# One lo in four of the first mixer's early weight chunks moved from VectorE to GpSimd

## The chip, the cores and the metric

The kernel runs on one core of one Trainium2 chip. The metric is the device time of one execution in microseconds (us); the time before is the median of three runs. The profile is one further execution, with its own time.

## What is computed

A trunk of two layers over 256 positions of width 2048, batch 1, all in float32. Layer 0 mixes tokens with gated DeltaNet heads and band attention behind one combined input projection; layer 1 with a Mamba-2 SSD. Each layer ends in a squared-ReLU MLP, and all norms are modulated by vectors made from `c`.

```python
def reference(x, c, mod_w, mod_b, norm_mix_w, norm_mlp_w, mlp_w1, mlp_w2, ab_w_in, ...):
    c_act = jax.nn.silu(c)
    for layer in range(DEPTH):
        mod = jnp.einsum('bd,de->be', c_act, mod_w[layer]) + mod_b[layer]
        sh1, sc1, g1, sh2, sc2, g2 = [m[:, None, :] for m in jnp.split(mod, 6, axis=-1)]
        h = rms_norm(x, norm_mix_w[layer]) * (1.0 + sc1) + sh1
        ...
        x = x + g1 * mix
        h = rms_norm(x, norm_mlp_w[layer]) * (1.0 + sc2) + sh2
        x = x + g2 * sq_relu_mlp(h, mlp_w1[layer], mlp_w2[layer])
    return x

def gdn_attn_mixer(h, w_in, ...):
    proj = jnp.einsum('btd,de->bte', h, w_in)
    gq, gk, gv, gz, gb, ga, aq, ak, av = split_sizes(proj, AB_SPLITS)
    ...
```

The change lies in the product `proj` of layer 0.

## The kernel before

Every weight comes in chunks of 128x2048 float32 (1 MB) into one of four buffers `raw`. A product at nearly full float32 precision is made of three matmuls of the fast type fp32r: each operand is split into hi (the value rounded to fp32r) and lo (the value minus hi), and hi by hi, hi by lo and lo by hi are summed. `split` (line 317) makes the two: hi (`wh`) is a cast on ScalarE (line 318), lo (`wl`) a subtraction of two SBUF tensors (line 319). `loader` (line 467) issues a chunk's DMA on the SP queue (line 477) and splits its two halves, `hf` 0 and 1, of 128x1024 each. A buffer `raw` is free again when lo of both halves is done. The halves' tiles `wh` and `wl` have four buffers each.

`b_item` (line 496) and `a_item` (line 522) are one chunk's work: load and split at once, its matmuls (line 309) one item later, first those of half 0, then those of half 1. In `b_item` the weights are the stationary operand, in `a_item` the activations `u`.

The first mixer's input projection begins at line 1422. The width of 2048 is taken in four quarters `kg`, and in each of the first three the loop at line 1484 runs over eight chunks, n = 0 to 7 (`kinds`, line 1422: six `b_item`, then two `a_item`). The partial results of n = 0 and 1 stay in PSUM over all quarters; those of n = 2 to 7 are copied out by ScalarE in kg 0 (line 1439) and in kg 1 and 2 added to what is there by VectorE (line 1441, one operand in PSUM). Quarter 3 follows in another order from line 1497, with the rest of the mixer around it.

Between the chunks the modulation of layer 0 is computed: `mod_job` (line 419) loads eight chunks `mraw` per quarter into the same four buffers, through the same SP queue (line 430), and VectorE multiplies each by `crow` and sums (line 433). At the end of a quarter `norm_unit` (line 737) makes the next quarter's activations from them: VectorE (line 750), ScalarE (line 752), VectorE (line 753). In quarter 2 ScalarE makes an undivided copy as well (line 755).

Each engine runs its instructions in the order that the program's scheduler has laid down; it goes by the order of the source and by priorities (`mod_job` lowers that of its product). GpSimd makes masks at the start and clears small tiles later.

Of the kernel before, what the change touches and what calls it, by code (L numbers as in the profile page):

```python
# [10 lines left out]
F32 = mybir.dt.float32  # L11
# [3 lines left out]
ALU = mybir.AluOpType  # L15
# [97 lines left out]
class Trunk:  # L113
# [200 lines left out]
    def tr(self, o, a, k=P):  # L314
        self.nc.tensor.transpose(o, a, self.ident[:k, :k])  # L315

    def split(self, src, hi, lo, pin=False):
        a = self.nc.scalar.copy(hi, src)  # L318
        b = self.nc.vector.tensor_tensor(lo, src, hi.bitcast(F32), op=ALU.subtract)  # L319
        if pin:  # L320
            self.tc.keep_in_program_order(a)
            self.tc.keep_in_program_order(b)
# [141 lines left out]
                return  # L464


    def loader(self, src, whole=False):

        nc = self.nc
        if self.ahead:  # L470
            res, self.ahead = self.ahead[1], None
            return (lambda: None), res
        res = []

        def load():
            raw = self.raw_p.tile([P, 2048], F32, tag="raw", name=self.nm("raw"))
            nc.sync.dma_start(raw, src)
            for hf in range(2):
                r = raw[:, 1024 * hf : 1024 * hf + 1024]
                if whole:  # L480
                    res.append((r, None))
                    continue
                wh = self.w_p.tile([P, 1024], F32R, tag="wh", name=self.nm("wh"))
                wl = self.w_p.tile([P, 1024], F32R, tag="wl", name=self.nm("wl"))
                self.split(r, wh, wl, self.pin > 0)
                res.append((wh, wl))
            self.pin -= 1

        return load, res
# [3 lines left out]

        return [[w and w.rearrange("p (k c) -> p k c", c=width) for w in half] for half in ws]

    def b_item(self, ps, src, act, first, last, after=None, whole=False):

        load, ws = self.loader(src, whole)

        def run():  # L500
            o_, (u, x) = ps(), act()
            for hf, (wh, wl) in enumerate(self.tiles(ws, 512)):
                for ct in range(4):
                    o = o_[ct // 2][:, ct % 2, :]
                    cs = slice(ct * P, ct * P + P)
                    for k in range(2):
                        ka = hf * 2 + k
                        st = first and ka == 0 and ct % 2 == 0
                        sp = last and ka == 3 and ct % 2 == 1
                        if whole:  # L510
                            self.mmx(o, wh[:, k, cs], x[hf][:, k], st, sp)
                            continue
                        self.mmx(o, wh[:, k, cs], u[hf][:, k, 0], st, False)
                        self.mmx(o, wh[:, k, cs], u[hf][:, k, 1], False, False)
                        self.mmx(o, wl[:, k, cs], u[hf][:, k, 0], False, sp)
                    if ct % 2:
                        yield

        self.emit(Item(load, run, after, self.still > 0))
        self.still -= 1  # L520

    def a_item(self, ps, src, act, first, last, after=None, whole=False):

        load, ws = self.loader(src, whole)
        flip = self.flip and not whole

        def run():
            o_, (u, x) = ps(), act()
            for hf, (wh, wl) in enumerate(self.tiles(ws, 512)):
                if flip:  # L530
                    for k in range(2):
                        ka = hf * 2 + k
                        st, sp = first and ka == 0, last and ka == 3
                        T = [slice(t * P, t * P + P) for t in range(2)]
                        for n in range(3):
                            for t in range(2):
                                self.mmx(o_[t], u[hf][:, k, n // 2, T[t]], (wh, wl, wh)[n][:, k], st and n == 0, sp and n == 2)
                        yield
                    continue
                for n in range(4):  # L540
                    k, t = (n % 2, n // 2) if last and hf else (n // 2, n % 2)
                    ka = hf * 2 + k
                    ts = slice(t * P, t * P + P)
                    st = first and ka == 0
                    sp = last and ka == 3
                    o = o_[t]
                    if whole:
                        self.mmx(o, x[hf][:, k, ts], wh[:, k], st, sp)
                    else:
                        self.mmx(o, u[hf][:, k, 0, ts], wh[:, k], st, False)  # L550
                        self.mmx(o, u[hf][:, k, 0, ts], wl[:, k], False, False)
                        self.mmx(o, u[hf][:, k, 1, ts], wh[:, k], False, sp)
                    if n % 2:
                        yield

        self.emit(Item(load, run, after, self.still > 0))
        self.still -= 1
# [828 lines left out]
    def run(self):  # L1386
# [14 lines left out]
        first = self.mod_job(0, (0, 1), range(0, 4), 2)  # L1401
        for n, _ in enumerate(first):
            if n == 5:
                r = self.norm_r()
# [11 lines left out]
        w = i["w_ab"]  # L1416
# [10 lines left out]
        def unit_now(kg):  # L1427
            if len(acts) <= kg:
                self.flush()
            return acts[kg]  # L1430

        def partial(n, ps):
            first = parts[n] is None
            if first:
                parts[n] = self.unit(shape=[P, 2, 512])
            for b in range(2):
                o = ps[b].rearrange("p f t -> p (f t)") if len(ps[b].shape) == 3 else ps[b]
                if first:
                    nc.scalar.copy(parts[n][:, b], o)
                else:  # L1440
                    nc.vector.tensor_tensor(parts[n][:, b], o, parts[n][:, b], op=ALU.add)  # L1441
                if b == 0:
                    yield

        def last(n, ps):
            c0, kind = kinds[n]
            part = parts[n]
            if kind:
                return self.att_qk(ps, self.knw if c0 == AK else self.qnw, part)
            return self.conv(ps, {GK: 8, GQ: 0, GV: 16}[c0 // 2 * 2] + 4 * (c0 % 2), self.gconv, None,  # L1450
                             None if part is None else part.rearrange("p a (f t) -> p (a f) t", f=2))

        def partial_item(kg, n, then=None):
            c0, kind = kinds[n]
            ps = held[n] if n < 2 else []

            def psum():
                if not ps and n < 2:
                    ps.extend([self.pm([P, 2, SEQ]), self.pm([P, 2, SEQ])])
                if not ps:  # L1460
                    self.room()
                    ps.extend(self.pg(kind > 0))
                return ps

            def after():
                if kg < 3:
                    if n >= 2:
                        self.evac(partial(n, ps))
                else:
                    tasks[n].task = self.evac(last(n, ps))  # L1470
                if then:
                    then()

            (self.a_item if kind else self.b_item)(psum, w[kg, c0], lambda: unit_now(kg), n >= 2 or kg == 0, n >= 2 or kg == 3, after, kg == 3 and n > 2)

        for kg in range(3):
            self.modgen = self.mod_job(0, (0, 1), range(4 * kg + 4, 4 * kg + 8), 2)
            self.rate = 0.5

            def then(kg=kg):  # L1480
                self.pump(100)
                self.q(self.norm_unit(self.R, kg + 1, mix0, acts, kg == 2))

            for n in range(8):
                partial_item(kg, n, then if n == 6 else None)
# [9 lines left out]
        self.prep = [Flag(), Flag()]  # L1495
        gdn = []
        partial_item(3, 0)
        partial_item(3, 1)
        self.a_block(w, AV, get, lambda ps: put("v0", self.att_v(ps)))
        partial_item(3, 2)  # L1500
# [39 lines left out]
        w = i["w_ssd"]  # L1540
# [116 lines left out]
```

## Time and profile before

| | us |
|---|---|
| three runs, median | 2752.32 |
| their lowest and highest | 2750.8, 2754.2 |
| the profiled execution | 2751.96 |
| its span in the profile | 2750.2 |
| TensorE, matmuls busy | 2678.6 (97%) |
| VectorE busy | 2154.5 (78%) |
| ScalarE busy | 1323.7 (48%) |
| GpSimd busy | 24.6 (1%) |

Busy times are shares of the span of one execution; they run beside each other. Two instructions of one engine can overlap at their edges, so a pair is shorter than twice one. PE is TensorE, PEld its weight loads, DVE VectorE, ACT ScalarE, POOL GpSimd, SPq the queue of SyncE, which issues loads. An entry in brackets, or behind the bar, is time in which the engine stood idle ahead of the instruction, and what released it. L319 is line 319.

### The profile page before, as it was taken

The numbers are of one execution on the slowest core, as the hardware profiler recorded it, in microseconds if no ns is written. First come the engines' busy times: TensorE is split into PE (matmuls) and PEld (weight loads), VectorE is DVE, ScalarE is ACT, GpSimd is POOL, SyncE is SP. The second block draws the span as 40 slices with busy tenths as digits, with TensorE's granted clock in tenths as the row PEclk, the third lists the DMA queues.
The fourth block names the chain that finished last, engine by engine and source line by source line (L and its number), as shares of the span: only waits on it lengthen the run. The fifth ranks groups of instructions, "written<-read, shape, count | busy, mean of one in ns | idle before, by whom it ended". The sixth has DMA issues, their size and how long they took to land.

```text
span 2750.2 us, 39612 instructions
## 1 busy us (share of the span) xinstructions
PE 2678.6 (97%) x15610; PEld 2341.0 (85%) x15610; DVE 2154.5 (78%) x3211; ACT 1323.7 (48%) x1841; POOL 24.6 (1%) x98
## 2 busy tenths in 40 slices
PE   5999999999999999999999999999999999999999
PEld 5887989878888888888788888888878888888888
DVE  7998998988888888777889876898777755555555
ACT  3444454445355354454555544555445354354452
POOL 1000000000000000000000000000000000000000
PEclk9999999999999999999999999999999999999999
DMA  9986487869888888887456565656557755555554
GB/s 345 351 322 238 158 317 274 310 235 348 307 323 303 318 301 306 303 305 273 179 197 206 210 214 199 235 193 219 196 186 287 275 192 191 184 185 192 190 188 134
DMA packets 99306, 680.06 MB, mean 247 GB/s; under 512 B 11056, under 2 KB 12336, under 8 KB 18224
## 3 DMA queue, kind: packets, MB, share of 16 engines
q1 hardware_dynamic: 94224, 669.07, 67.3%
q10 hardware_dynamic: 4896, 8.46, 1.0%
q8 instruction: 123, 2.02, 0.3%
q14 instruction: 63, 0.52, 0.1%
HBM read 675.33 MB, written 2.16 MB: 246 GB/s over the span
## 4 chain that ended last, share of the span: by engine, by line
PE 91%; DVE 6%; ACT 1%; issue 1%; DMA 1%; ACTq 0%; SPq 0%; DVEq 0%
PE pw L309 71%; PE pg L309 13%; PE pm L312 4%; PE pm L309 3%; DVE mraw L433 2%; DVE wl L319 1%; PE pm L315 1%; DVE hf L750 1%; DVE u L753 0%; DVE u L1441 0%; DVE x L791 0%; ACT pm L904 0%; ACT wh L318 0%; DMA x<-in_x_dram 0%; DMA sd_rowd<-sd_rows 0%
## 5 line engine op out<-in xcount | busy, mean ns | idle before, releaser
L309 PE MATMUL pw<-u,wh 128*128 128x512 f32 x5632 | 1746.1, 397 | 9.2 <-DVE u L753 5.5
L318 ACT CAST wh<-raw 128x1024 fp32r<-128x1024 f32 x870 | 910.7, 1053 | 1097.7 <-PE pw L309 818.1
L319 DVE TENSOR_TENSOR wl<-raw,wh 128x1024 fp32r<-128x1024 f32 x870 | 1054.6, 1222 | 410.8 <-ACT wh L318 361.7
L309 PE MATMUL pw<-u,wl 128*128 128x256 f32 x5632 | 1185.4, 281 | 1.3 <-DVE wl L319 1.3
L309 PEld LDWEIGHTS pw<-u,wh 128*128 128x128 f32 x5632 | 990.4, 189 | 170.0 <-issue 10.6
L309 PEld LDWEIGHTS pw<-u,wl 128*128 128x128 f32 x5632 | 966.9, 190 | 93.9 <-DVE wl L319 2.6
L433 DVE SCALAR_TENSOR_TENSOR mraw<-mraw,crow 128x2048 f32<-128x2048 f32 x192 | 438.9, 2287 | 33.3 <-DMA mraw<-in_mod_dram 33.1
L309 PE MATMUL pg<-wh,u 128*128 128x512 f32 x864 | 269.7, 396 | 0.0
L791 DVE SCALAR_TENSOR_TENSOR x<-pw,mod,x 128x256 f32<-128x256 f32 x352 | 161.5, 480 | 70.1 <-PE pw L309 67.3
L309 PEld LDWEIGHTS pg<-wh,u 128*128 128x128 f32 x864 | 161.3, 188 | 31.9 <-issue 0.5
L309 PE MATMUL pg<-wl,u 128*128 128x512 f32 x432 | 159.9, 394 | 0.7 <-DVE wl L319 0.5
L309 PE MATMUL pg<-u,wh 128*128 128x256 f32 x672 | 124.6, 285 | 0.0
L309 PEld LDWEIGHTS pg<-u,wh 128*128 128x128 f32 x672 | 105.7, 192 | 0.3
L309 PEld LDWEIGHTS pg<-wl,u 128*128 128x128 f32 x432 | 81.2, 188 | 17.6 <-DVE wl L319 1.8
L309 PE MATMUL pg<-u,wl 128*128 128x256 f32 x336 | 95.2, 283 | 0.0
L309 PE MATMUL pm<-u,wh 128*128 128x256 f32 x256 | 47.7, 290 | 19.2 <-ACT wh L318 19.2
L309 PEld LDWEIGHTS pg<-u,wl 128*128 128x128 f32 x336 | 64.4, 192 | 0.1
L846 DVE SCALAR_TENSOR_TENSOR u<-pad,cst,u 128x256 f32<-128x256 f32 x144 | 61.3, 481 | 1.9 <-ACT u L840 1.8
L319 DVE TENSOR_TENSOR u<-rl,u 128x512 fp32r<-128x512 f32 x64 | 44.2, 690 | 21.6 <-ACT u L318 21.6
L309 PEld LDWEIGHTS pm<-u,wh 128*128 128x128 f32 x256 | 41.0, 198 | 20.2 <-ACT wh L318 20.0
L752 ACT ACTIVATE u<-hf,mod 128x256 fp32r<-128x256 f32 x64 | 29.8, 505 | 56.2 <-DVE hf L750 56.2
L1355 ACT COPY rs<-pw 128x512 f32<-128x512 f32 x64 | 37.3, 583 | 31.8 <-PE pw L309 31.8
(279 smaller groups left out, 1508.6 us busy)
## 6 DMA issues: line engine op xcount, KB each, us to landing
raw<-in_w_dram SPq DMA_DIRECT2D x256, 1024.0 KB, 5.0
mraw<-in_mod_dram SPq DMA_DIRECT2D x192, 1024.0 KB, 5.5
raw<-in_w_ab_dram SPq DMA_DIRECT2D x56, 1024.0 KB, 5.8
raw<-in_w_ssd_dram SPq DMA_DIRECT2D x48, 1024.0 KB, 4.9
raw<-in_w_sz_dram SPq DMA_DIRECT2D x32, 1024.0 KB, 4.9
raw<-in_wo_ssd_dram SPq DMA_DIRECT2D x32, 1024.0 KB, 4.8
raw<-in_wo_ab_dram SPq DMA_DIRECT2D x16, 1024.0 KB, 5.6
sE<-sd_rowd ACTq DMA_DIRECT2D x32, 256.0 KB, 5.0
```

What stands on the lines that cost most here:

```text
L309: self.nc.tensor.matmul(o, a, b, start=start, stop=stop, skip_group_check=True)
L312: self.nc.tensor.matmul(o, lhsT, rhs, start=True, stop=True, skip_group_check=True)
L315: self.nc.tensor.transpose(o, a, self.ident[:k, :k])
L318: a = self.nc.scalar.copy(hi, src)
L319: b = self.nc.vector.tensor_tensor(lo, src, hi.bitcast(F32), op=ALU.subtract)
L433: x = nc.vector.scalar_tensor_tensor(raw, raw, 1.0, self.crow, op0=ALU.mult, op1=ALU.mult, accum_out=t[:, f : f + 1])
L750: nc.vector.scalar_tensor_tensor(h[:, f], self.x[cb][:, ff], scale[:, col], r, op0=ALU.mult, op1=ALU.mult)
L752: nc.scalar.activation(hi, h[:, f], AF.Identity, bias=shift[:, col])
L791: nc.vector.scalar_tensor_tensor(x[:, 2 * b + f], ps[:, f, n], g[:, 2 * cb + f : 2 * cb + f + 1], x[:, 2 * b + f], op0=ALU.mult, op1=ALU.add)
L846: nc.vector.scalar_tensor_tensor(h, pad[:, f, 1 + q : 257 + q], w[:, q, j : j + 1], h, op0=ALU.mult, op1=ALU.add)
L1355: nc.scalar.copy(lo, ps[:, :, 1])
```

## The change

In the quarters kg 0 to 2, for odd n, the subtraction that makes lo of the second half (hf 1) is issued on GpSimd and no longer on VectorE: four chunks in each quarter, twelve instructions in all. What is computed stays the same.

```diff
-    def split(self, src, hi, lo, pin=False):
+    def split(self, src, hi, lo, pin=False, pool=False):
         a = self.nc.scalar.copy(hi, src)
-        b = self.nc.vector.tensor_tensor(lo, src, hi.bitcast(F32), op=ALU.subtract)
+        b = (self.nc.gpsimd if pool else self.nc.vector).tensor_tensor(lo, src, hi.bitcast(F32), op=ALU.subtract)
...
-    def loader(self, src, whole=False):
+    def loader(self, src, whole=False, pool=False):
...
-                self.split(r, wh, wl, self.pin > 0)
+                self.split(r, wh, wl, self.pin > 0, pool and hf == 1)
...
-    def b_item(self, ps, src, act, first, last, after=None, whole=False):
-
-        load, ws = self.loader(src, whole)
+    def b_item(self, ps, src, act, first, last, after=None, whole=False, pool=False):
+
+        load, ws = self.loader(src, whole, pool)
...
-            (self.a_item if kind else self.b_item)(psum, w[kg, c0], lambda: unit_now(kg), n >= 2 or kg == 0, n >= 2 or kg == 3, after, kg == 3 and n > 2)
+            (self.a_item if kind else self.b_item)(psum, w[kg, c0], lambda: unit_now(kg), n >= 2 or kg == 0, n >= 2 or kg == 3, after, kg == 3 and n > 2, kg < 3 and n % 2 == 1)
```

`a_item` takes and passes `pool` as `b_item` does.

## Rows read from the trace of the kernel before

**Rows 1.** The page: engine totals, and the chain that ended last by engine.
```profile
PE 2678.6 (97%) x15610; PEld 2341.0 (85%) x15610; DVE 2154.5 (78%) x3211; ACT 1323.7 (48%) x1841; POOL 24.6 (1%) x98
...
PE 91%; DVE 6%; ACT 1%; issue 1%; DMA 1%; ACTq 0%; SPq 0%; DVEq 0%
```

**Rows 2.** Windows kg 0, 1, 2: length, engines' busy us (instructions), TensorE clock, DMA share, GB/s.
```profile
40.10:87.90 47.80, 47.68 (x336) 45.32 (x336) 39.73 (x46) 21.48 (x31) 0.00 (x0) 1.00 0.93 349
89.70:137.00 47.30, 46.16 (x336) 43.58 (x337) 45.51 (x54) 19.22 (x23) 0.00 (x0) 1.00 0.92 349
137.00:185.10 48.10, 46.44 (x338) 43.64 (x337) 47.46 (x60) 18.68 (x22) 0.00 (x0) 1.00 0.93 350
```

**Rows 3.** The chain in order of time, end of kg 2: start, us, what.
```profile
180.86 1.20 DVE u L1441 x2
...
186.76 11.29 PE pm L309 x92
```

**Rows 4.** VectorE's groups, 89.7 to 185.1 us: count, busy, mean ns, idle before.
```profile
L319 DVE TENSOR_TENSOR wl<-raw,wh 128x1024 fp32r<-128x1024 f32 x32 | 37.7, 1221 | 1.0 <-ACT wh L318 0.6 <-issue 0.3
L433 DVE SCALAR_TENSOR_TENSOR mraw<-mraw,crow 128x2048 f32<-128x2048 f32 x16 | 36.6, 2285 | 0.4 <-DMA mraw<-in_mod_dram 0.4
L1441 DVE TENSOR_TENSOR u<-pg,u 128x512 f32<-128x512 f32 x22 | 14.3, 684 | 1.0 <-PE pg L309 1.0
```

**Rows 5.** Timeline of TensorE: start, us, instructions, idle before and releaser.
```profile
89.79 0.74 PE L309 MATMUL pm<-u,wh 128*128 128x256 f32 x4 [1.72 <-ACT wh L318]
...
145.25 0.39 PE L309 MATMUL pm<-u,wl 128*128 128x256 f32 x1 [0.93 <-DVE wl L319]
...
186.76 0.39 PE L309 MATMUL pm<-u,wl 128*128 128x256 f32 x1 [1.00 <-DVE wl L319]
```

**Rows 6.** Waits of the SP queue, 40 to 200 us: total, times, longest.
```profile
SPq L477 <- DVE wl L319: 65.3, 22, 5.7
```

**Rows 7.** Timeline of VectorE in kg 2, around n = 3 and n = 5.
```profile
153.31 2.36 DVE L319 TENSOR_TENSOR wl<-raw,wh 128x1024 fp32r<-128x1024 f32 x2
155.59 2.28 DVE L433 SCALAR_TENSOR_TENSOR mraw<-mraw,crow 128x2048 f32<-128x2048 f32 x1
...
166.55 2.35 DVE L319 TENSOR_TENSOR wl<-raw,wh 128x1024 fp32r<-128x1024 f32 x2
168.82 1.28 DVE L1441 TENSOR_TENSOR u<-pg,u 128x512 f32<-128x512 f32 x2
```

**Rows 8.** Timeline of ScalarE: the casts of the same two chunks.
```profile
152.22 2.01 ACT L318 CAST wh<-raw 128x1024 fp32r<-128x1024 f32 x2 [5.03 <-DMA raw<-in_w_ab_dram]
...
163.38 2.00 ACT L318 CAST wh<-raw 128x1024 fp32r<-128x1024 f32 x2 [2.62 <-DMA raw<-in_w_ab_dram]
```

**Rows 9.** GpSimd's groups over the span, shapes kept apart.
```profile
L969 POOL MEMSET gY<- 128x512 f32 x24 | 12.4, 526 | 117.6 <-PE pm L312 45.5 <-ACT u L1067 40.5 <-DVE gPt L950 21.0
...
L391 POOL TENSOR_SCALAR Ucmask<-Ucmask 64x128 f32<-64x128 f32 x1 | 0.5, 536 | 0.0
...
L390 POOL COPY Ucmask<-Umask 128x128 f32<-128x128 f32 x1 | 0.3, 288 | 0.0
...
L1647 POOL MEMSET const-float32-1.0<- 128x1 f32 x1 | 0.1, 99 | 0.0
```

**Rows 10.** Timeline of GpSimd and VectorE at the start, in short windows.
```profile
4.60 1.01 POOL L402 TENSOR_SCALAR_AFFINE_SELECT lev<-lev 128x64 f32<-128x64 f32 x3
...
6.40 0.42 DVE L725 TENSOR_TENSOR ss<-ss,sq 128x256 f32<-128x256 f32 x1
6.42 0.50 POOL L401 TENSOR_SCALAR_AFFINE_SELECT lev<-lev 128x64 f32<-128x64 f32 x1
...
8.38 0.66 POOL L409 TENSOR_SCALAR_AFFINE_SELECT lev1T<-lev1T 128x64 f32<-128x64 f32 x1
8.41 0.49 DVE L725 TENSOR_TENSOR ss<-ss,sq 128x256 f32<-128x256 f32 x1
...
9.99 0.42 DVE L725 TENSOR_TENSOR ss<-ss,sq 128x256 f32<-128x256 f32 x1
```

More of the change, by code (lines that the diff above doesn't have):

```diff
@@ L520, in b_item, with a_item @@
         self.still -= 1
-    def a_item(self, ps, src, act, first, last, after=None, whole=False):
-        load, ws = self.loader(src, whole)
+    def a_item(self, ps, src, act, first, last, after=None, whole=False, pool=False):
+        load, ws = self.loader(src, whole, pool)
         flip = self.flip and not whole
```

## The prediction

> **What bounds the kernel now.** I read the first page for the whole (engine totals, the chain that ended last), then only the stretch that the change touches: the first three quarters of the first mixer's projections, kg 0 to 2, from about 40 to 187 us. Over the span TensorE is busy 97%, and 91% of the chain lies on it [rows 1]; so the question is what keeps TensorE waiting in those 147 us. The windows table, one row for each kg, shows little: 0.12, 1.14 and 1.66 us without a matmul, all at a granted clock of 1.00 [rows 2]. To that come two waits just outside the windows: 1.72 us at the seam of kg 0 and 1, and 1.00 us on lo at the seam of kg 2 and 3 [rows 5]. Sum 5.6 us, 0.2% of the kernel: **no relief in this stage can give more than 5.6 us**. The 1.72 us wait on a cast that stands behind the modulation and normalization work of the seam, so what belongs to the subtractions is nearer to 1.14 + 1.66 + 1.00 = 3.8 us.
>
> Who makes these waits? In kg 0 VectorE has room (39.73 busy of 47.80 us), in kg 1 and 2 it has almost none (45.51 of 47.30 and 47.46 of 48.10) [rows 2]. The chain runs over VectorE before it returns to TensorE at 186.76 [rows 3], the stalls at 145.25 and 186.76 name lo of VectorE as the releaser [rows 5], and the SP queue waits on the same subtractions for its free buffers: 65.3 us in 22 waits for weight loads [rows 6]. The DMA share is 0.92 to 0.93 [rows 2], so loads are close behind as the next limit. VectorE, TensorE and the loads thus run nearly level in kg 1 and 2; VectorE sets the pace by a hair.
>
> **What it removes.** Twelve subtractions (n = 1, 3, 5, 7 in three kg), each of 1.22 us by its row [rows 4]. Back to back they overlap: the pair at 166.55 is followed at 168.82, 2.27 us later [rows 7], so one is worth 1.135 us of VectorE's time. Eight lie in kg 1 and 2 (9.1 us), four in kg 0 (4.5 us, where VectorE already has 47.80 - 39.73 = 8.1 us free and TensorE is the bound: worth nothing). Casts, loads and matmuls stay; ScalarE still makes every hi.
>
> **What it adds.** Twelve GpSimd subtractions of 128x1024, an operation the trace of before does not have. Bounds from GpSimd's rows [rows 9]: a 128x1 memset takes 0.099 us, a 128x512 memset 0.526, so writing alone costs (526 - 99)/511 = 0.84 ns a column; 1024 of them and the start make 0.95 us, the lower end. The 64x128 scalar operation takes 0.536: 3.44 ns a column, 3.6 us, the upper end. Between them: a copy of 128x128 takes 0.288, which is 1.49 ns, so one read adds 0.65 ns; a second read makes 2.14 ns and 2.3 us for 1024 columns. I take 2.3, because the copy is the nearest row (read and write of full partitions, no constant) and the subtraction only adds one more stream.
>
> Can TensorE wait for the later lo? For n = 3 of kg 2 both casts are ready at 152.22 + 2.01 = 154.2 [rows 8]; the subtraction on GpSimd would end at 156.5, or about 158.8 if it first has to let a 2.2 us VectorE operation pass. VectorE's own pair of before ended at 153.31 + 2.36 = 155.67 [rows 7], and the second half is needed half an item after the first: kg 2 has 8 items in 46.44 us of matmuls [rows 2], so 2.9 us. So it about fits, and the raw buffer comes free up to 3 us later than now; for chunks whose pair was queued (n = 5: ready at 163.38 + 2.00 = 165.4 [rows 8], pair only ended at 168.9 [rows 7]) GpSimd is no later than VectorE was. Nothing else stands in GpSimd's queue: it has no instruction in any of the three windows [rows 2].
>
> **What it makes VectorE pay.** The open term. Beside each other the two engines do disturb each other in the trace [rows 10]. Three GpSimd selects at 4.60, with VectorE nearly idle, take 1.01 us together, 0.34 each; beside VectorE's two-input adds the one at 6.42 takes 0.50 and ends at 6.92, 0.1 us after the add of 6.40 has ended, and the one of 8.38 takes 0.66 and ends 0.14 after the add of 8.41. The other way, that add takes 0.49, with a select begun just before it, against 0.42 undisturbed (9.99). That is the picture of two engines that take turns, not of two that run through. The selects read only 64 columns, so the price for 1024 is not in a row; it lies between nothing and the whole 2.3 us (or 3.6), and I take the whole 2.3 for every VectorE operation that has two inputs in SBUF, since the rows show one engine's end following the other's.
>
> The Trainium skill's page "SBUF — State Buffer" (section "Who interferes with whom") says it more strongly: a VectorE instruction with two SBUF inputs and a GpSimd instruction that reads SBUF exclude each other for a whole instruction. The trace agrees as far as the 0.1 us between those ends goes; no row of before shows it for a long one. By that rule alone each moved subtraction takes VectorE more time than it frees.
>
> What is covered: the accumulation of partial sums (line 1441) reads PSUM and one SBUF operand. After the pair of n = 5 come two of these [rows 7], and after that of n = 7 as well, 1.20 us by the chain [rows 3]; I count them as running on under a GpSimd operation. After the pairs of n = 1 and 3 comes a 2.28 us modulation product with two SBUF inputs [rows 7], which would be held.
>
> **The sum**, kg 1 and 2: four operations (n = 1, 3) cost 2.3 - 1.135 = +1.15 each, +4.6; four (n = 5, 7) cost 2.3 - 1.2 - 1.135 = about -0.05 each, -0.2. Of the +4.4 VectorE's own waits swallow a part: of 1.0 us before the accumulations, 0.6 before subtractions and 0.4 before a product, 2.0 in all [rows 4], I take 1.5, as the accumulations' waits lie behind n = 3. Kg 0: four times 1.15 = 4.6 against 8.1 us free: nothing. Left: **+2.9 us**. Behind the stage TensorE is busy without a break worth the name, so the delay reaches the end. The profiled execution took 2751.96 us (span 2750.2), the median of three is 2752.32, 0.4 us more; 2751.96 + 2.9 = 2754.9, by the median 2755.2. I give 2755.
>
> **Rivals.** *No turn-taking.* The engines run beside each other, VectorE's demand in kg 2 falls from 47.5 to 42.9 us, below TensorE's 46.4, and TensorE becomes the bound: -3.8 us at most, I put it at -3, 2749 us. For it: the add of 6.40 lasted 0.42 beside a select, as if alone. Against it: the selects' ends [rows 10]. Even with the seam's 1.72 us it gives 2746.8, just at the bound below. *Slower: the full price.* The place is VectorE's queue in kg 1 and 2. If no accumulation runs on under a GpSimd operation, the sum is 8 x 1.15 - 1.5 = +7.7 us, 2760; if GpSimd needs its upper 3.6 us and the cover holds, 4 x 2.47 + 4 x 1.27 - 1.5 = +13.4 and kg 0 adds 4 x 2.47 - 8.1 = +1.8: 2767. With the cover it passes 0.2% (5.5 us) once an operation holds VectorE for 2.6 us or longer (8p - 13.9 = 7.0). For it: the 3.44 ns row; against: that row uses 64 partitions and a constant. *The move does little*, since GpSimd finds no gap in a full VectorE queue and only gets in where VectorE waits or accumulates: VectorE then loses about as little as it gained, and second halves come late by one modulation product (2.2 us), inside the half item. About 0 us, inside the forecast's band.
>
> **How the numbers follow.** A measurement of this kernel tells about 0.2%, 5.5 us, from no change. Turn-taking with cover, or little effect, -1.5 to +5.5 us: 0.44. No turn-taking, -1.5 us and below: 0.23, of which 0.04 goes below -5.5. Full price, over +5.5 us: 0.33, of which 0.05 goes over +12. So faster 0.04, same 0.44 + 0.19 = 0.63, slower 0.33. The range from 2748 (the -3.8 of no turn-taking) to 2764 leaves out about 0.05 above, where the 3.6 us end lies, and 0.07 below.
>
> **What would show it.** GpSimd: 12 new rows; near 2.3 us or well above it. VectorE's subtractions: 12 fewer in the three windows, and products or subtractions beside GpSimd whose mean rises above 2.29 and 1.22 us by one to two us: then turns are taken; if the means stay, the first rival holds. Windows: kg 0 stays at 47.8 us, kg 1 and 2 grow by 1 to 2 us each; TensorE's waits on lo name POOL or DVE. I am wrong if accumulations stretch too, if kg 0 grows, or if the time moves after 190 us, for which nothing here gives a reason.

## The result and the profile after

| | before | after |
|---|---|---|
| median of five runs, us | 2752.32 | 2765.52 |
| their lowest and highest | 2750.8, 2756.2 | 2763.17, 2769.27 |
| the profiled execution, us | 2751.96 | 2763.89 |
| its span | 2750.2 | 2761.8 |

The ratio after to before is 1.0047, 95% interval 1.0032 to 1.0061: 13 us slower (9 to 17). The profiled executions differ by 11.9 us, and the sums below go by these. Of the runs behind all times below, three at 3794 to 4448 us, with a lower granted clock, are left out of the ratios. The forecast was +2.9 us, its range ended at 2764, and the full-price rival stood at 2760.

The page of the kernel after, engine totals and the chain that ended last, against [rows 1]:

```profile
PE 2681.1 (97%) x15610; PEld 2343.8 (85%) x15610; DVE 2160.5 (78%) x3199; ACT 1320.3 (48%) x1841; POOL 59.5 (2%) x110
...
PE 90%; DVE 7%; ACT 1%; DMA 1%; issue 1%; SPq 0%; ACTq 0%; DVEq 0%
```

Twelve instructions have left VectorE, twelve have come to GpSimd, and VectorE is 6 us **busier** than before. The windows of kg 0, 1 and 2 (length, busy us of PE, PEld, DVE, ACT, POOL, TensorE's clock, DMA share, GB/s), against [rows 2]:

```profile
40.10:86.90 46.80, 46.77 (x335) 44.26 (x334) 41.39 (x40) 20.78 (x30) 12.48 (x4) 0.97 0.89 334
89.20:140.30 51.10, 47.27 (x333) 44.55 (x334) 47.07 (x51) 19.31 (x24) 11.52 (x4) 0.97 0.90 333
140.30:195.20 54.90, 48.63 (x339) 45.45 (x338) 49.69 (x56) 17.90 (x23) 11.24 (x4) 0.97 0.80 296
```

The windows are cut by eye. Measured from a matmul of one quarter to the same matmul of the next, the three took 49.37, 47.26 and 48.45 us before and 49.64, 51.02 and 54.63 after: +0.3, +3.8 and +6.2, 10.2 in all. TensorE now stands idle for 3.8 and 6.3 us in the windows of kg 1 and 2, where it stood for 1.14 and 1.66; at the beginning of kg 3 TensorE is 9.5 us later than before, and at the end of the span 11.6.

The groups of GpSimd (whole stretch) and of VectorE (89.2 to 195.2 us; count, busy, mean ns, idle before), against [rows 4]:

```profile
L319 POOL TENSOR_TENSOR wl<-raw,wh 128x1024 fp32r<-128x1024 f32 x12 | 35.2, 2937 | 142.9 <-ACT wh L318 142.9
...
L433 DVE SCALAR_TENSOR_TENSOR mraw<-mraw,crow 128x2048 f32<-128x2048 f32 x16 | 40.0, 2502 | 0.0
L319 DVE TENSOR_TENSOR wl<-raw,wh 128x1024 fp32r<-128x1024 f32 x25 | 32.0, 1304 | 1.1 <-ACT wh L318 1.1
L1441 DVE TENSOR_TENSOR u<-pg,u 128x512 f32<-128x512 f32 x22 | 14.1, 681 | 8.0 <-PE pg L309 8.0
L753 DVE SCALAR_TENSOR_TENSOR u<-hf,mod,u 128x256 fp32r<-128x256 f32 x7 | 7.3, 1082 | 0.0
```

Two things are to be seen. Products, subtractions and line 753 have longer means (2502 against 2285 ns, 1304 against 1221, 1082 against 480 in the run below where nothing is held), while the accumulations of line 1441 kept theirs (681 against 684). And VectorE waits 8.0 us for TensorE ahead of the accumulations, 1.0 before.

The timelines of GpSimd and VectorE of the kernel after, put together in four places (start, us, what, idle before and releaser):

```profile
116.10 1.28 DVE L1441 TENSOR_TENSOR u<-pg,u 128x512 f32<-128x512 f32 x2
116.49 2.40 POOL L319 TENSOR_TENSOR wl<-raw,wh 128x1024 fp32r<-128x1024 f32 x1 [8.62 <-ACT wh L318]
117.30 3.74 DVE L433 SCALAR_TENSOR_TENSOR mraw<-mraw,crow 128x2048 f32<-128x2048 f32 x1
...
130.05 2.28 DVE L433 SCALAR_TENSOR_TENSOR mraw<-mraw,crow 128x2048 f32<-128x2048 f32 x1
131.48 3.10 POOL L319 TENSOR_TENSOR wl<-raw,wh 128x1024 fp32r<-128x1024 f32 x1 [12.59 <-ACT wh L318]
132.38 2.23 DVE L441 TENSOR_TENSOR mod<-mod,cst 128x2 f32<-128x2 f32 x1
...
158.73 2.49 POOL L319 TENSOR_TENSOR wl<-raw,wh 128x1024 fp32r<-128x1024 f32 x1 [13.37 <-ACT wh L318]
161.57 1.29 DVE L1441 TENSOR_TENSOR u<-pg,u 128x512 f32<-128x512 f32 x2 [2.60 <-PE pg L309]
...
184.48 2.39 POOL L319 TENSOR_TENSOR wl<-raw,wh 128x1024 fp32r<-128x1024 f32 x1 [10.21 <-ACT wh L318]
184.63 4.39 DVE L433 SCALAR_TENSOR_TENSOR mraw<-mraw,crow 128x2048 f32<-128x2048 f32 x1
```

At 131.48 GpSimd begins while a product of VectorE still runs (130.05 to 132.33), and takes 3.10 us; a VectorE instruction of 128x2, at most 0.16 us otherwise, lasts 2.23. At 184.48 the product ends 2.1 us late. At 116.49 the accumulations run on beside GpSimd at full speed and only the product behind them is held, by 1.46. At 158.73 VectorE was just ending a subtraction and then idle until 161.57, and nothing was held. Each releaser of GpSimd is ScalarE's cast: it starts when hi is there, **wherever VectorE's queue is just then**.

For a balance I add up, over the VectorE timeline, what each instruction lasted beyond the median of its kind in the same run (**held**), and VectorE's idle time. Held: 7.2 us in kg 0, 12.1 in kg 1 and 2. Freed there: 8 x 1.135 = 9.1. Net +3.0. VectorE's idle time in kg 1 and 2: 9.2 us against 2.4 before, +6.8. Together +9.8, against the 9.9 by which kg 1 and 2 grew (3.76 + 6.18). This is a ledger of VectorE's time; what causes what is left to the experiments.

### The profile page after: what moved, and what is told of

Read it like the earlier page. It is cut to its first block, busy times and chain, and to the rows that moved or that the text cites. A ratio compares the mean times of both kernels' runs of the same rounds, so it can differ in the third digit from the quotient of the medians.

```text
span 2761.8 us, 39619 instructions
## 1 busy us (share of the span) xinstructions
PE 2681.1 (97%) x15610; PEld 2343.8 (85%) x15610; DVE 2160.5 (78%) x3199; ACT 1320.3 (48%) x1841; POOL 59.5 (2%) x110
## 4 chain that ended last, share of the span: by engine, by line
PE 90%; DVE 7%; ACT 1%; DMA 1%; issue 1%; SPq 0%; ACTq 0%; DVEq 0%
PE pw L309 70%; PE pg L309 12%; PE pm L312 4%; PE pm L309 3%; DVE mraw L433 2%; DVE wl L319 1%; PE pm L315 1%; DVE u L753 1%; DVE hf L750 0%; DVE x L791 0%; DVE u L1441 0%; ACT wh L318 0%; DMA mraw<-in_mod_dram 0%; ACT pm L904 0%; DMA raw<-in_w_ab_dram 0%
## 5 line engine op out<-in xcount | busy, mean ns | idle before, releaser
L319 DVE TENSOR_TENSOR wl<-raw,wh 128x1024 fp32r<-128x1024 f32 x858 | 1043.8, 1226 | 411.2 <-ACT wh L318 361.0
L433 DVE SCALAR_TENSOR_TENSOR mraw<-mraw,crow 128x2048 f32<-128x2048 f32 x192 | 446.8, 2328 | 31.8 <-DMA mraw<-in_mod_dram 31.5
L309 PEld LDWEIGHTS pg<-wl,u 128*128 128x128 f32 x432 | 81.2, 188 | 19.3 <-DVE wl L319 3.5
```

Source lines behind the costliest of these rows:

```text
L309: self.nc.tensor.matmul(o, a, b, start=start, stop=stop, skip_group_check=True)
L319: b = (self.nc.gpsimd if pool else self.nc.vector).tensor_tensor(lo, src, hi.bitcast(F32), op=ALU.subtract)
L433: x = nc.vector.scalar_tensor_tensor(raw, raw, 1.0, self.crow, op0=ALU.mult, op1=ALU.mult, accum_out=t[:, f : f + 1])
```

## The experiments

"Old order" means that VectorE, ScalarE and TensorE (and GpSimd where it has more than these instructions) are held, by edges that order issue without a wait, to the order of the kernel before, the moved instructions left out; "new order" is that of the kernel after. Each was run 5 to 11 times; ratios are to the kernel before, run beside it on the same chip.

| kernel | median, us | ratio, 95% interval |
|---|---|---|
| twelve moved, old order | 2759.9 | 1.0025, 1.0016 to 1.0034 |
| none moved, new order | 2755.17 | 1.0005, 0.9996 to 1.0014 |
| twelve left out, GpSimd only writes, new order | 2752.7 | 0.9995, 0.9986 to 1.0003 |
| the same, old order | 2751.14 | 0.9988, 0.9979 to 0.9997 |
| none moved, twelve extra on GpSimd | 2772.54 | 1.0069, 1.0056 to 1.0083 |
| kg 0's four moved, old order | 2752.9 | 1.0003, 0.9993 to 1.0012 |
| n = 5, 7 of kg 1, 2 moved, old order | 2756.29 | 1.0012, 1.0003 to 1.0020 |
| the same four, a copy behind them | 2755.57 | 1.0010, 1.0000 to 1.0019 |
| the same four, begun behind lo of half 0 | 2752.43 | 0.9999, 0.9990 to 1.0008 |
| twelve moved, in pieces, old order | 2763.24 | 1.0034, 1.0021 to 1.0047 |

The same ledger for each, from its one profiled execution, in us: the length of kg 0 and of kg 1 and 2 together (matmul to matmul), and for kg 1 and 2 what was held, what was freed (1.135 for each subtraction that left VectorE) and VectorE's idle time.

| kernel | kg 0 | kg 1 and 2 | held | freed | idle |
|---|---|---|---|---|---|
| before | 49.4 | 95.7 | 0 | 0 | 2.4 |
| after | 49.6 | 105.7 | 12.1 | 9.1 | 9.2 |
| twelve moved, old order | 50.8 | 102.6 | 15.9 | 9.1 | 2.9 |
| none moved, new order | 49.8 | 97.4 | 0 | 0 | 4.0 |
| twelve left out, new order | 49.4 | 94.8 | 0 | 9.1 | 9.9 |
| the same, old order | 49.4 | 92.5 | 0 | 9.1 | 7.6 |
| none moved, twelve extra | 51.7 | 110.6 | 17.3 | 0 | 0.6 |
| kg 0's four moved | 50.6 | 96.9 | 0 | 0 | 3.9 |
| n = 5, 7 moved | 49.9 | 100.8 | 6.7 | 4.5 | 5.1 |
| the same, a copy behind them | 49.6 | 99.4 | 7.4 | 4.5 | 3.3 |
| the same, begun behind lo of half 0 | 49.0 | 98.9 | 5.2 | 4.5 | 4.8 |
| twelve moved, in pieces | 51.3 | 101.7 | 8.3 | 9.1 | 8.6 |

One execution says less than the medians: runs of one kernel lie 5 to 12 us apart, and the profiled execution was the fastest of its kernel's runs for "none moved, new order" and "twelve extra", and the slowest for "begun behind lo of half 0".

### The order apart from the move

VectorE's order in kg 1 and 2 is not that of before: relieved of instructions, the scheduler placed the rest anew. The timeline of VectorE around n = 2 of kg 1, in the kernel before:

```profile
106.81 2.29 DVE L433 SCALAR_TENSOR_TENSOR mraw<-mraw,crow 128x2048 f32<-128x2048 f32 x1 [0.36 <-DMA mraw<-in_mod_dram]
...
109.03 0.68 DVE L1441 TENSOR_TENSOR u<-pg,u 128x512 f32<-128x512 f32 x1
```

And in the kernel after:

```profile
104.38 1.23 DVE L319 TENSOR_TENSOR wl<-raw,wh 128x1024 fp32r<-128x1024 f32 x1
109.11 1.29 DVE L1441 TENSOR_TENSOR u<-pg,u 128x512 f32<-128x512 f32 x2 [3.51 <-PE pg L309]
110.31 2.28 DVE L433 SCALAR_TENSOR_TENSOR mraw<-mraw,crow 128x2048 f32<-128x2048 f32 x1
```

The accumulations now stand ahead of the product. TensorE isn't through with what they add, so VectorE waits 3.51 us; the chunk of the product behind them landed at 107.09, so for the last 2.0 us of the wait there was ready work. VectorE's and ScalarE's orders also differ in places in the first 22 us of kg 3; from there on they are as before.

The move with the old order:

```diff
-        self.mlp(1, self.norm(("mlp", 1)))
+        self.mlp(1, self.norm(("mlp", 1))); hold_order(self)
...
+def hold_order(trunk):
...
+    for text in ORDERS.values():
...
+            trunk.tc.add_manual_dep(traced[f"I-{n}"], f"I-{p}", mybir.DependencyInfo(mybir.DependencyClass.NoSync, mybir.DependencyReason.DATA), reason="order")
```

> The twelve lo stay on GpSimd, but VectorE, ScalarE and TensorE are held to the order of the kernel before (less the twelve). Theory order (of the 13 us lost, the held VectorE work makes about 3 and the new order, in which accumulations stand ahead of products and VectorE waits 8.0 us for TensorE in place of 1.0, most of the rest): 2755 to 2758 us, VectorE's waits for TensorE in the stage back at 1 to 2 us. Theory lock (the held work makes all of it, whatever the order): within 2 us of the changed kernel, 2763 to 2768, the waits on lo as long as there.

And the other half, the new order with all subtractions on VectorE (`split` as before, `hold_order` with the lists of the kernel after):

```diff
-        b = (self.nc.gpsimd if pool else self.nc.vector).tensor_tensor(lo, src, hi.bitcast(F32), op=ALU.subtract)
+        b = self.nc.vector.tensor_tensor(lo, src, hi.bitcast(F32), op=ALU.subtract)
```

> Every lo on VectorE as before, no GpSimd work, but all engines held to the order of the changed kernel, each of the twelve behind its sibling of half 0. Theory order: 2756 to 2760 us, VectorE waiting 5 to 8 us for TensorE ahead of accumulations. Theory lock: 2751 to 2754, as before.

With the old order: +6.7 us by the medians (2759.9 against 2753.25), interval +4.4 to +9.4. Its VectorE timeline beside GpSimd:

```profile
157.61 3.33 POOL L319 TENSOR_TENSOR wl<-raw,wh 128x1024 fp32r<-128x1024 f32 x1 [8.07 <-ACT wh L318]
158.60 4.49 DVE L433 SCALAR_TENSOR_TENSOR mraw<-mraw,crow 128x2048 f32<-128x2048 f32 x1
...
170.06 3.46 POOL L319 TENSOR_TENSOR wl<-raw,wh 128x1024 fp32r<-128x1024 f32 x1 [9.12 <-ACT wh L318]
171.18 2.62 DVE L753 SCALAR_TENSOR_TENSOR u<-hf,mod,u 128x256 fp32r<-128x256 f32 x1
...
182.44 2.40 POOL L319 TENSOR_TENSOR wl<-raw,wh 128x1024 fp32r<-128x1024 f32 x1 [8.92 <-ACT wh L318]
182.53 4.46 DVE L433 SCALAR_TENSOR_TENSOR mraw<-mraw,crow 128x2048 f32<-128x2048 f32 x1
```

Each of the eight subtractions of kg 1 and 2 holds one VectorE instruction, seven by 2.07 to 2.21 us and one, which found VectorE idle for the rest, by 0.72: 15.9 in all, less 9.1 freed makes **+6.8**, and kg 1 and 2 grew by 6.9. No accumulation gave cover. VectorE's idle time is back at 2.9 us (1.1 of it for TensorE), so no new wait of size is needed for the sum. (Kg 0 took 1.5 us more in this execution as well; I come to it below.)

With the new order alone: +1.9 us, which its interval (-1.1 to +3.9) doesn't tell from nothing. So neither half alone makes the 13 us. In the profiles the new order costs kg 1 and 2 something each time: 1.7 us with nothing moved (97.4 against 95.7), 2.3 with the relief alone (94.8 against 92.5, next section) and 3.1 with the move (105.7 against 102.6). The last saved 3.8 us of holding (12.1 against 15.9) and paid 6.3 us of idling (9.2 against 2.9). In the whole time the kernel after and the old order differ by 4.6 us of the profiles and 6 of the medians, and their intervals overlap at the edge (1.0032 to 1.0034); what comes behind the stage I take up below.

### Relief without the lock

Lo of the twelve halves is left out (zeros): GpSimd writes it with a memset and writes a scratch of 128x1499, 2.3 us of writing in all, and it reads one column before and one after. VectorE is relieved as by the change.

```diff
-        b = (self.nc.gpsimd if pool else self.nc.vector).tensor_tensor(lo, src, hi.bitcast(F32), op=ALU.subtract)
+        b = blank(self, src, hi, lo) if pool else self.nc.vector.tensor_tensor(lo, src, hi.bitcast(F32), op=ALU.subtract)
...
+    keep(g.tensor_copy(scr[:, :1], hi.bitcast(F32)[:, :1]))
+    keep(g.memset(scr[:, 1:], 0.0))
+    keep(g.memset(lo.bitcast(F32), 0.0))
+    return keep(g.tensor_copy(scr[:, :1], src[:, :1]))
```

With the new order:

> The changed kernel in its own order, but GpSimd only writes for as long as a subtraction (a 128x1499 and a 128x1024 memset between two copies of one column): lo of the twelve halves is left out (zeros). VectorE has nothing that it must yield to. Theory lock: no VectorE operation is stretched and the time is at or below that of before, 2748 to 2753 us. Theory order: the stretching is gone too, but the waits of VectorE for TensorE stay and the time is 2755 to 2760.

With the old order:

> VectorE relieved of all twelve lo (left out: zeros, written by GpSimd, which reads only single columns) in the order of the kernel before. It shows the most that the relief can give. If VectorE set the pace (prediction): 2748.5 to 2750.5. If TensorE and the loads are as late without it: within 1.5 us of the kernel before, 2751 to 2754.

Measured -0.5 and -2.7 us. GpSimd is busier in the stage than in the kernel after, and no VectorE instruction is held; the windows of kg 1 and 2 of the second:

```profile
90.21:135.66 45.45, 45.45 (x339) 43.56 (x337) 41.19 (x51) 17.99 (x21) 14.24 (x16) 1.00 0.97 364
135.66:182.67 47.01, 45.95 (x339) 43.66 (x337) 43.63 (x57) 20.13 (x26) 16.26 (x16) 1.00 0.91 343
```

So GpSimd's **writing** holds nothing; what the subtraction has beyond it are its reads of SBUF. And 9 us of VectorE's time given back for nothing are worth 2.7 us (0.8 to 5.8). TensorE then has no idle time left in kg 1.

The -0.5 us of the new order (interval -3.9 to +0.8) isn't told from nothing, nor from the -2.7. Its accumulations wait for TensorE too, though nothing is held and TensorE is within 0.1 us of where it was before; this is the place at which the kernel after waited 3.51:

```profile
108.23 1.29 DVE L1441 TENSOR_TENSOR u<-pg,u 128x512 f32<-128x512 f32 x2 [2.49 <-PE pg L309]
```

### The lock alone

All subtractions stay on VectorE, and GpSimd does twelve extra ones of two constant tensors, once hi is there; nobody reads the results.

```diff
-                self.split(r, wh, wl, self.pin > 0, pool and hf == 1)
+                self.split(r, wh, wl, self.pin > 0); pool and hf == 1 and extra(self, wh)
...
+    keep(g.tensor_copy(scr[:, :1], hi.bitcast(F32)[:, :1]))
+    keep(g.tensor_tensor(scr, trunk.crow[:, :1024], trunk.crow[:, 1024:], op=ALU.subtract))
```

> The kernel before in its own order, with twelve further GpSimd subtractions of 128x1024 from constants whose result nobody reads, each started when hi of the same half is there. VectorE is relieved of nothing. If the engines take turns for whole instructions, about 2 us per GpSimd operation that finds VectorE at work: eight in kg 1 and 2 make +9 to +16 us, kg 0 hides its four: 2761 to 2768. If VectorE keeps a share of the way to SBUF, its operations stretch by less than half and the time is below 2758. If nothing is shared: 2752.

Measured +19.3 us. Nothing waits for these instructions and nothing was freed, so this is the price of holding by itself: 17.3 us held in kg 1 and 2, all eight by 2.07 to 2.22. Its groups of GpSimd and the windows of kg 1 and 2:

```profile
L1663 POOL TENSOR_TENSOR scr<-crow 128x1024 f32<-128x1024 f32 x12 | 39.9, 3327 | 1.1 <-POOL scr L1662 0.2
...
92.25:146.23 53.98, 49.26 (x337) 46.39 (x337) 53.63 (x55) 17.76 (x20) 15.16 (x8) 0.94 0.82 298
146.23:202.87 56.64, 48.11 (x339) 43.75 (x337) 56.43 (x61) 20.00 (x26) 18.40 (x8) 1.00 0.82 301
```

VectorE is busy for 53.63 of 53.98 and 56.43 of 56.64 us: it is the bound. Of the 17.3 us held, 1.8 came out of its idle time (0.6 us left of 2.4), and kg 1 and 2 took 14.9 longer.

### Where the free time is: kg 0 alone

```diff
-            (self.a_item if kind else self.b_item)(psum, w[kg, c0], lambda: unit_now(kg), n >= 2 or kg == 0, n >= 2 or kg == 3, after, kg == 3 and n > 2, kg < 3 and n % 2 == 1)
+            (self.a_item if kind else self.b_item)(psum, w[kg, c0], lambda: unit_now(kg), n >= 2 or kg == 0, n >= 2 or kg == 3, after, kg == 3 and n > 2, kg < 1 and n % 2 == 1)
```

> Only the four of kg 0 on GpSimd, all other lo on VectorE in the order of before. Theory free (the prediction's: VectorE has 8 us to spare in kg 0 and TensorE sets the pace): 2752 to 2754 us. Theory seam (the modulation products held in kg 0 make the seam of kg 0 and 1 late, as kg 0 was 1.5 us longer in the run with twelve in the old order): 2754 to 2756.

Measured +0.4 us (-1.9 to +3.3), not told from nothing. VectorE was held 7.5 us in kg 0, where it has 8.6 us of idle time. In the profile it is not quite free: kg 0 took 50.6 us against 49.4, and TensorE waited longer at the seam behind it than the 1.72 us of before [rows 5].

```profile
89.56 0.74 PE L309 MATMUL pm<-u,wh 128*128 128x256 f32 x4 [2.86 <-ACT wh L318]
```

The other runs that hold VectorE in kg 0 have a longer wait there too: 2.33 us in the kernel after, 3.21 with the old order. So a price of about 1 us at the seam stands in the profiles, below what the times can tell.

### The cover

Only the four subtractions that the prediction counted as covered (n = 5, 7 of kg 1 and 2), first as they come. The edit is that of the last kernel, with this condition in the same place:

```diff
+            (self.a_item if kind else self.b_item)(psum, w[kg, c0], lambda: unit_now(kg), n >= 2 or kg == 0, n >= 2 or kg == 3, after, kg == 3 and n > 2, 0 < kg < 3 and n in (5, 7))
```

> The same four operations in the same order of VectorE, without the copy: GpSimd starts as soon as hi is there. Both theories: each operation holds one VectorE operation by about 2.1 us, 4 x (2.15 - 1.135) = +4.1 us: 2756 to 2759. If instead the place of the start makes no difference, the time is that of the run with the copy.

Then with a copy of one column of half 0's lo on GpSimd, meant to make its subtraction begin only when VectorE has done half 0, with the accumulations next in VectorE's queue:

```diff
+                pool and hf == 1 and after_lo(self, res[0][1]); self.split(r, wh, wl, self.pin > 0, pool and hf == 1)
...
+    trunk.tc.keep_in_program_order(trunk.nc.gpsimd.tensor_copy(trunk.scr, lo.bitcast(F32)[:, :1]))
```

> Only n = 5 and 7 of kg 1 and 2 on GpSimd (four operations), VectorE in the order of the kernel before less these four, and GpSimd held back by a one-column copy until VectorE has finished lo of half 0, so that it starts together with the two accumulations that read PSUM. Theory cover (an accumulation runs on beside GpSimd; the prediction failed since GpSimd starts at the cast, at another place of VectorE's queue): the accumulations keep 0.6 us each, the operation behind them is held by 1.0 to 1.3 us in place of 2.1, and the sum is 4 x (1.15 - 1.135) = 0: 2752 to 2755 us. Theory no cover (the accumulations are held as well): 2.1 us each, +4 us, 2756 to 2759.

The second missed its aim: the scheduler put the copy *behind* the subtraction, as its timeline shows.

```profile
115.83 2.73 POOL L319 TENSOR_TENSOR wl<-raw,wh 128x1024 fp32r<-128x1024 f32 x1 [106.78 <-ACT wh L318]
116.22 2.61 DVE L753 SCALAR_TENSOR_TENSOR u<-hf,mod,u 128x256 fp32r<-128x256 f32 x1
...
120.43 0.19 POOL L1661 COPY scr<-wl 128x1 f32<-128x1 f32 x1 [1.88 <-DVE wl L319]
```

So both are the same experiment, four that start at the cast: +3.8 and +3.1 us, against 4 x (2.15 - 1.135) = 4.1. The agreement is partly luck. In each run one of the four did meet accumulations and held only 0.41 or 1.00 us, so holding less freed makes +2.2 and +2.9, and VectorE's idle time rose by 2.8 and 0.9. I ran it once more with the subtraction kept behind the copy (`self.pin > 0 or pool` in the call of `split`):

> As the run with the copy was meant: n = 5 and 7 of kg 1 and 2 on GpSimd, and now the copy does stand ahead of the subtraction in GpSimd's queue, so that this starts when VectorE has finished lo of half 0 and turns to two accumulations. Theory cover: the accumulations keep 0.6 us each beside GpSimd, the product behind them is held by 1.0 to 1.5 us, the sum is about 0: 2751 to 2754 us, and 3 us less than without the copy. Theory no cover: a VectorE operation is held by 2.1 us each time and the time stays at 2755 to 2758.

```profile
120.91 2.41 POOL L319 TENSOR_TENSOR wl<-raw,wh 128x1024 fp32r<-128x1024 f32 x1
121.03 1.29 DVE L1441 TENSOR_TENSOR u<-pg,u 128x512 f32<-128x512 f32 x2 [0.34 <-PE pg L309]
122.24 3.23 DVE L433 SCALAR_TENSOR_TENSOR mraw<-mraw,crow 128x2048 f32<-128x2048 f32 x1
...
182.46 1.28 DVE L1441 TENSOR_TENSOR u<-pg,u 128x512 f32<-128x512 f32 x2
182.74 2.42 POOL L319 TENSOR_TENSOR wl<-raw,wh 128x1024 fp32r<-128x1024 f32 x1
183.66 3.65 DVE L433 SCALAR_TENSOR_TENSOR mraw<-mraw,crow 128x2048 f32<-128x2048 f32 x1
```

Now the accumulations run through under GpSimd (1.28 us as ever), and the product behind is held for what is left, 0.95 to 1.50. That is near the prediction's term for n = 5 and 7 (2.3 - 1.2 = 1.1 held): 5.2 us for the four, 0.6 more than freed, where the two runs above held 6.7 and 7.4. The time doesn't move (ratio 0.9999), but its interval overlaps that of the run without the copy (1.0008 and 1.0003). And in the one profiled execution kg 1 and 2 took 98.9 us, 3.2 more than before and only 0.5 and 1.9 less than in the two runs: VectorE's idle time was 4.8 us, and 3.4 us of kg 1 ran at a granted clock of 0.50. So the cover is shown in the rows, the gain in time is not.

### Shorter turns

Each subtraction as four instructions of 256 columns, so that VectorE is held only for a piece:

```diff
+    for c in (slice(n, n + 256) for n in range(0, 1024, 256)):
+        b = trunk.tc.keep_in_program_order(trunk.nc.gpsimd.tensor_tensor(lo[:, c], src[:, c], hi.bitcast(F32)[:, c], op=ALU.subtract))
```

> All twelve on GpSimd in the old order, each as four instructions of 256 columns. If the way to SBUF is held for one instruction at a time, no VectorE operation is held by more than one piece, 0.6 to 0.8 us, before it gets its turn, GpSimd takes longer (4 to 8 us for a half, as it waits for VectorE between pieces), and what VectorE loses in all stays near 2 us for each half: 2758 to 2763 us. If GpSimd keeps the way over all four pieces, one operation is held by over 2 us as before. If VectorE slips through between pieces at little loss (under 1 us for each half): 2750 to 2756.

Measured +10.8 us, worse than whole ones. Its GpSimd timeline, TensorE's wait for it from 42 to 196 us and that of the SP queue from 40 to 200 us (total, times, longest):

```profile
162.43 4.95 POOL L1662 TENSOR_TENSOR wl<-raw,wh 128x256 fp32r<-128x256 f32 x4 [6.96 <-PE pg L309]
...
PE pg L309 <- POOL wl L1662: 3.7, 5, 1.0
...
SPq L477 <- POOL wl L1662: 48.3, 10, 5.8
```

VectorE is held by 0.2 to 0.55 us a time, 8.3 in kg 1 and 2, less than the 9.1 freed. But the waiting has changed sides: a piece that meets a 2.28 us product waits it out, the four take 4.95 to 7.42 us together, and lo comes late. TensorE waits for it directly, and through the loads: a buffer is free only when lo is done, so the SP queue waits 88.5 us for subtractions (48.3 and 40.2 for VectorE's) in place of 65.3 [rows 6], and the casts wait 57.9 us for loads where they waited 42.3. VectorE's idle time in kg 1 and 2 rose to 8.6 us: a shorter turn gave its time back, and lo and the buffers came late instead.

## Why the prediction was wrong, point by point

**The bound: right.** "No relief in this stage can give more than 5.6 us", nearer 3.8, and -3 for the rival without turn-taking. Relief for nothing measured -2.7.

**GpSimd's 2.3 us: nearly right.** 2.39 to 2.52 undisturbed, 2.94 in the mean with its own waits for VectorE (up to 5 us).

**Turn-taking for the whole instruction: right**, and it was the open term. The Trainium skill's page "SBUF — State Buffer" (section "Who interferes with whom") says that the shared port pair is an exclusive lock, which the first comer keeps for its whole instruction; the trace agrees: the rows at 131.48 (3.10 us for GpSimd, 2.23 for a 128x2 instruction) show both directions, and the page's condition, only against a GpSimd instruction that reads SBUF, agrees with the memset runs, where nothing was held.

**Accumulations run on: right** (681 against 684 ns).

**Kg 0 free: right within what the times can tell** (+0.4 us, -1.9 to +3.3). The prediction's own sign of being wrong, a longer kg 0, did show in the profiles: +1.2 us with kg 0's four alone, +1.5 with the old order, +0.3 in the kernel after, by a longer wait at the seam.

**What is covered: wrong, and this is the first step that failed.** "After the pair of n = 5 come two of these ... I count them as running on under a GpSimd operation." The accumulations do stand there [rows 7], but GpSimd does not begin when VectorE's pair would have stood: it begins with the cast [rows 8]. I had even written that for n = 5 the cast was done 3.5 us before VectorE's pair ended, and used it for lateness only. GpSimd so runs up to these 3.5 us earlier, beside a product, a subtraction or line 753. Covered: none of the four with the old order, one in the kernel after. The term of -0.05 each is about +1.0 each (2.15 - 1.135): with the old order n = 5 and 7 cost about +4 us where the sum has -0.2, and the whole time rose by 6.7 where it has 2.9. The rival at full price, +7.7, came near, though by two misses against each other: its 9.2 were 6.8, and the 1.5 that it took off were +0.5. Tied to the place in the queue, cover came much as worked out (0.95 to 1.50 held for 1.1).

In the kernel after itself this miss doesn't show in the sum of holding, and that is luck: n = 5 and 7 cost +3.2 us for -0.2, but both operations of n = 3 ran while VectorE was idle and held nothing, so n = 1 and 3 cost -0.2 for the +4.6 forecast. Net +3.0 for the +4.4 of the prediction.

**"VectorE's own waits swallow a part", 1.5 us: wrong in sign, the second step that failed, and the larger miss in the kernel after.** It took the order behind as fixed. The order was laid anew by the scheduler, with accumulations ahead of products, and VectorE's idle time in kg 1 and 2 rose by 6.8 us where I let it fall by 1.5. With the old order it stayed (+0.5). Part of this comes with the order itself: with the relief and nothing held, the accumulation that waited 3.51 us waited 2.49, and the new order made kg 1 and 2 longer by 1.7 to 3.1 us in each of three pairs of profiles (in the times +1.9 alone, not told from nothing). Part may be that a held lo delays TensorE and the accumulation then waits for it: at the other two long waits, 2.60 and 1.65 us, TensorE stood 5.0 and 9.6 us later than before. The rows show both waits (7.1 us on lo, 8.0 on TensorE); the shares aren't separated.

The waits of the kernel after in the stage:

```profile
PE pg L309 <- DVE wl L319: 7.1, 4, 2.6
...
DVE u L1441 <- PE pg L309: 8.0, 4, 3.5
...
SPq L477 <- DVE wl L319: 51.0, 21, 4.6
SPq L477 <- POOL wl L319: 13.4, 5, 4.4
```

TensorE's waits name lo of **VectorE**, not of GpSimd: the moved halves come in time, the halves that stayed come late. Weight loads wait 64.4 us for subtractions in place of 65.3 [rows 6], so the later release of the moved halves doesn't show there, as predicted.

**"Behind the stage ... the delay reaches the end", and nothing after 190 us: partly wrong.** 9.5 us of lag stand at the beginning of kg 3, 12.2 at about 500 us, 11.6 at the end. All engines' orders are the same there as before. With the old order the lag is 7.5, 9.0 and 7.3 at the same three points, so such shifts come and go; what made the 2.1 us of the kernel after last isn't settled.

What the runs make of the 12 to 13 us: about 6.7 for more held than freed, 2 to 3 more in the stage for the new order, and 2 to 3 behind the stage without a shown cause. The first is shown; the second rests on single profiles and on times that hardly tell it. No version tried that computes lo is told to be faster than the kernel before.

## What to carry to other kernels

Before an instruction goes from VectorE to GpSimd, set what it frees against what it holds: here 1.135 us freed and 2.15 held, a loss where VectorE is the bound. It cost little only where VectorE was idle or at work that GpSimd doesn't hold. GpSimd runs when its input is ready and not at the old place in VectorE's queue, so a cover has to be tied to it by a dependence. And compare the issue order of the relieved engine before and after: a scheduler that places instructions by time will place the ones that stayed anew.

## What the runs showed of the hardware

- A VectorE instruction of 128x2, 0.16 us at most alone, took 2.23 us beside a GpSimd subtraction. The price goes by GpSimd's instruction, not by VectorE's.
- TensorE's clock fell after two waits. Three windows of the kernel after, the first with the wait on lo (2.84 us from the start of the last matmul to that of the next):

```profile
173.20:176.14 2.94, 0.38 (x4) 0.18 (x2) 2.94 (x4) 1.99 (x2) 1.07 (x1) 0.99 0.80 312
176.14:179.50 3.36, 3.36 (x15) 3.36 (x16) 3.36 (x5) 0.00 (x0) 0.00 (x0) 0.50 0.63 217
179.50:182.90 3.40, 3.40 (x31) 3.40 (x30) 2.27 (x2) 1.05 (x1) 0.00 (x0) 1.00 0.92 323
```

In the second it did 15 matmuls at a granted clock of 0.50 (1.2 GHz), in the third 31 at 1.00 (2.4 GHz). The wait at the seam of kg 0 and 1, 2.72 us from the start of the last matmul to the next, was also followed by a low stretch (0.71 from 89.26 to 92.66 us); before, the same seam had 2.11 us and stayed at 1.00. The 15 matmuls from 176.14 on took 3.36 us, before the same 15 took 1.80: part of the stage's price, which no term of the prediction had.

The length of the wait alone doesn't decide it. With twelve moved in the old order TensorE stood idle for 2.80 us ahead of 150.68, and the clock stayed at 1.00. In the run begun behind lo of half 0 the seam's wait was 1.72 us, as before, and two us later came this stretch:

```profile
91.86:95.27 3.41, 3.41 (x19) 3.41 (x18) 3.41 (x5) 1.96 (x3) 0.00 (x0) 0.50 0.76 267
```
